# Seven block products in more chunks of a gated feed-forward net, with the activations dealt and turned in contiguous runs

## The chip, the cores and the metric

One core of one Trainium2 chip runs the whole program. The metric is the device time of one execution in microseconds (us). The core has TensorE (PE: matrix products; PEld: the loading of its stationary operand), VectorE (DVE), ScalarE (ACT), GpSimd (POOL) and SyncE (SP, which here only issues DMAs).

## The reference

Two layers; each is a gated feed-forward net, a mixer, cross attention and a second net, each followed by a layer norm. The change touches the four nets (two per layer).

```
D_MODEL = 1024; SEQ = 256; DEPTH = 2; D_FF = 2816

def swiglu(x, w_gate, w_up, w_down):
    return (jax.nn.silu(x @ w_gate) * (x @ w_up)) @ w_down

for l in range(DEPTH):
    h = layer_norm(ALPHA * h + 0.5 * swiglu(h, ffn1_gate[l], ffn1_up[l], ffn1_down[l]), ...)
    ...                                   # mixer: w_in, recurrence, convolution, pooling, w_out
    h = layer_norm(ALPHA * h + mix, ...)
    h = layer_norm(ALPHA * h + cross_attn(h, mem, ca_q[l], ca_k[l], ca_v[l], ca_o[l]), ...)
    h = layer_norm(ALPHA * h + 0.5 * swiglu(h, ffn2_gate[l], ffn2_up[l], ffn2_down[l]), ...)
```

## The kernel before

**Products in three parts.** All data is fp32. Each operand is split into a high part (a cast on ScalarE, line 61, to the type that TensorE takes) and a low part (a subtraction on VectorE, line 62), and a product is the sum of three matmuls: high by high, high by low, low by high (`mm_rows`, lines 130 to 133; every matmul is recorded at line 106). The activations of the net's input stand transposed in `xT` (1024 rows in 8 groups of 128, by 256 tokens), as high and low parts.

**A net in chunks.** `ffn` works through the 2816 hidden columns in five chunks of 512 and a last one of 256 (loop at line 639). A weight tile `raw` holds 1 MB (three of them); `load` fetches it with one DMA from SyncE and splits it in two halves into `whi` and `wlo`, of which there are eight each. An ordinary chunk (`hidden`, line 484) takes two gate and two up loads, so 8 halves, and 96 matmuls of 512 columns; the two token tiles i = 0, 1 get accumulators of their own among four `acc` banks. Then `activate` (ScalarE, line 402) writes SiLU of the gate sums into `sg`, and `gated` (VectorE, line 406) multiplies by the up sums.

**Dealing and turning.** The product with w_down needs the activations transposed. `turn` (line 411) deals `sg` with four DMAs over 32-partition bands into the tile `dealt` (line 415, one buffer), so that VectorE's transposes of 32x32 blocks (line 418, one per token tile) finish the job; then `ah` and `al` take the high and low part. In the transposes both sides are read and written in steps of four elements:

```
nc.vector.transpose(
    d.rearrange("p k (i b) -> p b k i", b=4), x[:, :, i, :].rearrange("p b (j k) -> p b k j", k=4)
)
```

To match this order of rows, w_down is fetched "strewn" (row 4p + k to partition p), save for the last chunk.

**Slabs.** w_down comes in slabs of two 128-row groups (`both`, line 631): 24 matmuls of 512 columns into the four `dn` accumulators, two slabs per chunk. In the loop over c, after chunk c's own products, the second slab of chunk c-2 and the first of chunk c-1 are done. So one slab stands ahead of chunk 2, two stand ahead of chunks 3, 4 and 5. The last slabs are done in `finish`, together with the layer norm.

**The chunk made by seven block products.** In three of the four nets, chunk 3 is made by `by_seven` (line 515): gate and up weights of the chunk, stacked, times the two token tiles form a product of 2 x 2 blocks, which the seven-product scheme of Winograd does with 7 x 12 = 84 matmuls in place of 96, and more additions. `w00` and `w01` are the upper halves of the gate and up weights, `w10` and `w11` the lower halves. The sums w00+w01, w00+w11, w01+w11 and w00+w10 are made in place on VectorE (line 544), each half then split like any weight: 14 halves in all. The sums of x's blocks are made once per net (`blocks_of_x`, line 497) in the tile `spare`, and split into the tiles `kTh` and `kTl`; the same `spare` later takes w00. w01 lies in the tiles of the layer norm's parameters (`lng`, `lnb`), w11 and w10 in two `raw` tiles. The results of the products are combined on VectorE by `put` (line 566). The first net has no such chunk (`early`: its `ffn` pool also builds masks and loads the memory).

**Order.** A planner orders each engine's instructions by priority (the order of the program text) and by its own estimate of when operands and tiles are free; each engine then runs its list in order, each instruction waiting for what it needs. DMA issues on SyncE are such a list too.

**Transposes on TensorE.** `transposed` (line 173) transposes the layer norm's result with an identity matrix `idn` as one operand; after ffn1 the second token tile is reversed with `jdn`.

Of the kernel before, what the change touches and what calls it, by code (L numbers as in the profile page):

```python
# [46 lines left out]
def model(ctx: ExitStack, tc: tile.TileContext, t: dict, out: bass.AP):  # L47
# [16 lines left out]
    def load(src, k0, nk, c0, ncol, fine=False, strewn=False):  # L64

# [4 lines left out]
        for a in range(k0, k0 + nk, step):  # L70
# [4 lines left out]
            for b in range(0, step, part):  # L75
                loads.append(nc.sync.dma_start(
                    raw[:, b : b + part, :],
                    src[:, c0 : c0 + ncol].rearrange("(p k) c -> p k c", p=P)[:, a + b : a + b + part, :]
                    if strewn
                    else src[(a + b) * P : (a + b + part) * P, c0 : c0 + ncol].rearrange("(k p) c -> p k c", p=P),  # L80
                ))
# [71 lines left out]

    jdn = cst.tile([P, P], F32, name="jdn")
# [24 lines left out]
    def load_memory(mp, behind):  # L179
        m = [mp.tile([P, 4, 8, 32], F32, tag="m", name="m", bufs=2) for _ in range(2)]  # L180
# [23 lines left out]
    rows = cst.tile([P, P], F32, name="rows")  # L204
# [10 lines left out]
    def small_parameters(op):  # L215
        nc.gpsimd.memset(rows, 0.0)
# [13 lines left out]
        mf = op.tile([P, NT, len(narrow), 64], F32, name="mf", bufs=1)  # L230
# [61 lines left out]
    def finish(mm, y, scale, gb, last=False, flip=False):  # L292
# [6 lines left out]
        for i in range(NT):  # L299
# [8 lines left out]
            for c in pieces:  # L308
# [6 lines left out]
                else:  # L315
                    mm(
                        i, n, slice(0, 512), None,
                        None if last or not i or not n else lambda: transposed(h[0], 0, xTh, xTl),
# [21 lines left out]
        return lambda: transposed(h[1], 1, xTh, xTl, jdn if flip else idn)  # L340

    def project_back(slabs, late, gb, scale, between=lambda: None):
# [30 lines left out]
        return finish(tail, y, scale, gb)  # L373


    def ffn(l, name, n, pend=None, last=False, early=None):
        gate, up, down = (t[f"{name}_{x}"][l] for x in ("gate", "up", "down"))
        with tc.tile_pool(name="ffn", bufs=2, reuse_waits="tile") as fp:
# [21 lines left out]

            def activate(s, i, og):
                nc.scalar.activation(halves(s[:, i, :]), sums(og), AF.Silu)

            def gated(s, i, ou):
                v = halves(s[:, i, :])
                nc.vector.tensor_tensor(v, sums(ou), v, op=ALU.mult)
# [4 lines left out]
            def turn(s):  # L411
# [4 lines left out]
                for i in range(NT):  # L416
                    d = fp.tile([P, 4, P], F32, tag="up", name="square")
                    nc.vector.transpose(  # L418
                        d.rearrange("p k (i b) -> p b k i", b=4), x[:, :, i, :].rearrange("p b (j k) -> p b k j", k=4)
                    )  # L420
                    split(ah[:, :, tok(i)], al[:, :, tok(i)], d)
                return ah, al

            def first():
# [5 lines left out]
                if pend is None:  # L430
# [8 lines left out]
                    with tc.manual_schedule(engines={E.Activation, E.DVE, E.PE}):  # L439
# [8 lines left out]
                        transposed_half(h[0], 0, 0, xTh, xTl)  # L448
                        busy(1)
                        split(*wg.todo[0])  # L450
                        transposed_half(h[0], 0, 1, xTh, xTl)
# [3 lines left out]
                        transposed_half(h[1], 1, 0, xTh, xTl)  # L455
                        group(1, 0)
                        split(*wg.todo[2])
                        transposed_half(h[1], 1, 1, xTh, xTl)
# [56 lines left out]
            def by_seven(c0, bx):  # L515
                def quarter(m, j, halves_of):
                    for b, r in enumerate(halves_of):
                        n = r.shape[1]
                        k = 4 * j + b * n
                        loads.append(nc.sync.dma_start(  # L520
                            r, m[k * P : (k + n) * P, c0 : c0 + CHUNK].rearrange("(k p) c -> p k c", p=P)
                        ))
                    return [r[:, 2 * h : 2 * h + 2, :] for h in range(2) for r in halves_of[:1]] if n == 4 else halves_of

# [3 lines left out]
                def raw():  # L528
                    return rows_by_columns(wp.tile([P, 2048], F32, tag="raw", name="raw", bufs=3))

                w00 = quarter(gate, 0, [rows_by_columns(
                    fp.tile([P, 4, 4 * P], F32, tag="spare", name="sum", bufs=1).rearrange("p n c -> p (n c)")
                )])
                w01 = quarter(up, 0, [
                    rows_by_columns(wp.tile([P, DM], F32, tag=g, name="raw")) for g in ("lng", "lnb")
                ])
                w11 = quarter(up, 1, [raw()])
                w10 = quarter(gate, 1, [raw()])

                def parts_of(r, plus=None):  # L540
                    hi, lo = [], []
                    for i in range(2):
# [4 lines left out]
                        h, w = (x.rearrange("p (k c) -> p k c", c=CHUNK) for x in (h, w))  # L547
# [14 lines left out]
                def half_sum():  # L562
                    return halves(fp.tile([P, 4, P], F32, tag="up", name="half").rearrange("p k t -> p (k t)"))

                def put(o, a, op, b):
                    nc.vector.tensor_tensor(o, a, b, op=op)

                s = activations()
                g = [halves(s[:, i, :]) for i in range(NT)]
                o = [acc((P, CHUNK)) for _ in range(4)]  # L570
                run(o[0], part_of_x(0, 0), parts_of(w00))
                nc.scalar.copy(g[0], sums(o[0]))
# [3 lines left out]
                put(e, sums(o[1]), ALU.add, g[0])  # L576
                run(o[3], bx[2], parts_of(w01, w11))
                put(g[1], sums(o[3]), ALU.add, e)
                f = half_sum()
                put(f, sums(o[2]), ALU.subtract, g[1])  # L580
                put(e, sums(o[2]), ALU.subtract, e)
# [561 lines left out]
```

## Time and profile before

| | |
|---|---|
| median of 3 runs | 1081.59 us (1081.54 to 1081.89) |
| profiled execution: its time / its span | 1082.44 / 1080.7 us |
| PE busy | 1071.4 us (99%), 6015 matmuls |
| VectorE busy | 908.4 us (84%), 1198 instructions |
| ScalarE busy | 592.8 us (55%) |
| GpSimd busy | 61.0 us (6%) |
| DMA | 231.86 MB, 215 GB/s in the mean |
| mean granted TensorE clock | 0.998 |

The span runs from the first to the last instruction of the profiled execution; its own time has 1.74 us more. "Busy" counts instructions that run, also while matmuls overlap; a matmul of 512 columns is recorded with 380 ns, while the next starts 216 ns after it. In rows of groups the columns are: line, engine, operation, output<-inputs, shape, count, busy us, mean ns of one, and the engine's idle time ahead of them with what ended it. In the chain of work and the timelines a row is: start, duration, engine, line, and xcount of merged instructions.

### The profile page before, as it was taken

The page shows a single profiled execution, that of the slowest core. Times are in us where ns is not written, and L with a number is a line of the kernel's source. Part 1 is how long each engine was busy: PE and PEld are TensorE (multiplying, and loading weights), DVE is VectorE, ACT ScalarE, POOL GpSimd, SP SyncE. Part 2 cuts the span into 40 slices and gives each one's busy share as a digit, 9 for nine tenths or more (in the row PEclk, how much of TensorE's full clock was granted, in tenths as well). Part 3 has the DMA queues.
Part 4 walks back from the last instruction along what each step waited for, and adds up shares of the span by engine and source line. Part 5 has one row for each costly group of instructions (what it writes and reads, how often), then busy time and mean ns, then how long its engine had stood idle before and what let it go on. Part 6 is the DMA issues. An engine that isn't in the chain of part 4 may idle for free.

```text
span 1080.7 us, 15689 instructions
## 1 busy us (share of the span) xinstructions
PE 1071.4 (99%) x6015; PEld 947.5 (88%) x6015; DVE 908.4 (84%) x1198; ACT 592.8 (55%) x828; POOL 61.0 (6%) x113
## 2 busy tenths in 40 slices
PE   9999999999999999999999999999999999999997
PEld 7888888989899888888888888898898998888886
DVE  6678677998988898998697998798989889889885
ACT  6456553766457455556365465456764664645650
POOL 9500001000000000000000000010000000000000
PEclk9999999999999999999999999999999999999999
DMA  9986764754476387288468459656536664773761
GB/s 325 289 293 203 249 223 153 237 196 165 167 263 204 123 295 269 96 275 286 156 234 282 166 166 329 229 165 241 174 122 231 240 228 154 255 253 109 260 236 39
DMA packets 122715, 231.86 MB, mean 215 GB/s; under 512 B 6352, under 2 KB 45552, under 8 KB 117520
## 3 DMA queue, kind: packets, MB, share of 16 engines
q1 hardware_dynamic: 120848, 228.48, 63.1%
q0 software_dynamic: 1216, 1.20, 0.4%
q10 hardware_dynamic: 576, 1.18, 0.3%
q8 instruction: 47, 0.77, 0.3%
q14 instruction: 28, 0.23, 0.1%
HBM read 216.15 MB, written 1.05 MB: 201 GB/s over the span
## 4 chain that ended last, share of the span: by engine, by line
PE 99%; DMA 0%; DVE 0%; issue 0%; DVEq 0%
PE acc L106 65%; PE dn L106 30%; PE acc L170 1%; PE dn L845 1%; DMA h<-in_x_dram 0%; PE dn L904 0%; PE dn L903 0%; PE dn L893 0%; PE acc L969 0%; PE dn L810 0%; PE dn L437 0%; DVE h L334 0%; DVE h L330 0%; DVE st L322 0%; DVE h L314 0%
## 5 line engine op out<-in xcount | busy, mean ns | idle before, releaser
L62 DVE TENSOR_TENSOR wlo<-raw,whi 128x1024 fp32r<-128x1024 f32 (+1 forms) x390 | 460.8, 1207 | 91.0 <-ACT whi L61 81.1
L61 ACT CAST whi<-raw 128x1024 fp32r<-128x1024 f32 (+1 forms) x390 | 391.2, 1040 | 258.3 <-PE dn L106 128.4
L106 PE MATMUL acc<-whi,xT 128*128 128x512 f32 x1192 | 359.7, 380 | 0.0
L106 PEld LDWEIGHTS acc<-whi,xT 128*128 128x128 f32 x1192 | 225.2, 189 | 32.1
L106 PE MATMUL acc<-wlo,xT 128*128 128x512 f32 x596 | 225.9, 379 | 0.0
L106 PE MATMUL acc<-xT,whi 128*128 128x512 f32 x576 | 142.1, 382 | 0.0
L106 PE MATMUL dn<-whi,ah 128*128 128x512 f32 x346 | 131.5, 380 | 0.0
L106 PE MATMUL dn<-wlo,ah 128*128 128x512 f32 x346 | 131.2, 379 | 0.0
L106 PE MATMUL dn<-whi,al 128*128 128x512 f32 x346 | 131.1, 379 | 0.0
L106 PEld LDWEIGHTS acc<-wlo,xT 128*128 128x128 f32 x596 | 112.7, 189 | 15.7
L106 PEld LDWEIGHTS acc<-xT,whi 128*128 128x128 f32 x576 | 104.1, 190 | 11.8
L106 PE MATMUL dn<-whi,xT 128*128 128x512 f32 x288 | 88.8, 382 | 0.0
L106 PEld LDWEIGHTS acc<-xT,wlo 128*128 128x128 f32 x576 | 75.5, 191 | 3.9
L106 PE MATMUL acc<-xT,wlo 128*128 128x256 f32 x576 | 75.9, 275 | 0.0
L106 PEld LDWEIGHTS dn<-wlo,ah 128*128 128x128 f32 x346 | 65.4, 189 | 9.5 <-DVE wlo L62 0.3
L106 PEld LDWEIGHTS dn<-whi,al 128*128 128x128 f32 x346 | 65.4, 189 | 9.3
L106 PEld LDWEIGHTS dn<-whi,ah 128*128 128x128 f32 x346 | 65.4, 189 | 9.1
L418 DVE STREAM_TRANSPOSE square<-dealt 128x512 f32<-128x512 f32 x40 | 62.8, 1645 | 3.8 <-DMA dealt<-sg 3.8
L327 POOL TENSOR_TENSOR rs<-rs,nhalf 128x1 f32<-128x1 f32 x16 | 14.9, 928 | 846.3 <-DVE rs L326 846.3
L106 PEld LDWEIGHTS dn<-whi,xT 128*128 128x128 f32 x288 | 54.7, 190 | 7.8 <-DVE xT L62 0.3
L106 PE MATMUL dn<-wlo,xT 128*128 128x512 f32 x144 | 54.8, 381 | 0.0
L61 ACT CAST ah<-square 128x512 fp32r<-128x512 f32 x40 | 24.6, 619 | 39.7 <-DVE square L418 39.7
(227 smaller groups left out, 1174.0 us busy)
## 6 DMA issues: line engine op xcount, KB each, us to landing
raw<-in_ffn_down_dram SPq DMA_DIRECT2D x44, 1024.0 KB, 5.4
raw<-in_ffn_up_dram SPq DMA_DIRECT2D x41, 1024.0 KB, 6.1
raw<-in_ffn_gate_dram SPq DMA_DIRECT2D x39, 1024.0 KB, 5.1
raw<-in_w_in_dram SPq DMA_DIRECT2D x24, 1024.0 KB, 5.0
dealt<-sg SPq DMA_DIRECT2D x80, 128.0 KB, 3.8
raw<-in_ca_k_dram SPq DMA_DIRECT2D x8, 1024.0 KB, 4.9
raw<-in_w_out_dram SPq DMA_DIRECT2D x8, 1024.0 KB, 4.8
raw<-in_ca_v_dram SPq DMA_DIRECT2D x8, 1024.0 KB, 5.4
```

What stands on the lines that cost most here:

```text
L61: nc.scalar.copy(hi, src)
L62: lows.append(nc.vector.tensor_tensor(lo, src, hi.bitcast(F32), op=ALU.subtract))
L106: nc.tensor.matmul(o, w, x, start=start, stop=stop)
L170: nc.tensor.transpose(pt[:, k, :], src[:, (4 * j + k) * P : (4 * j + k + 1) * P], unit)
L327: nc.gpsimd.tensor_tensor(rs, rs, nhalf[:, 0:1], op=ALU.pow)
L418: nc.vector.transpose(d.rearrange("p k (i b) -> p b k i", b=4), x[:, :, i, :].rearrange("p b (j k) -> p b k j", k=4))
L845: nc.tensor.matmul(o[g, hh, :], kc[:, hh, g], x, start=True, stop=True)
```

## The change

- Chunks 2 and 4 of three nets, and chunk 4 of the first, are made by `by_seven`; x's blocks are made at chunk 1 (in the first net at chunk 3). LN parameters are fetched after the last such chunk.
- `activate` and `gated` work in two instructions of 256 columns per token tile, in an order that needs no steps afterwards. `turn`'s transposes read and write contiguous runs of 32.
- A permuted identity `pdn` (one copy on GpSimd at the start) is used for the transposes ahead of each net's input and output, so that tokens come in the matching order. w_down is no longer strewn; the last chunk's split carries the permutation in its steps.
- In `by_seven`, w00 lies in the tiles `spare0` and `spare1`, w10 in `dealt` and `spare2` (each half with a DMA of its own), w11 in the one `raw` tile. w11's own product now comes fifth, ahead of the two with w10. SiLU and gating come at the end, into a new tile in `spare2`.
- Rows and masks of the small parameters, and the memory's tiles, move into `spare2`, `spare0` and `spare1`.

```
+    pdn = cst.tile([P, P], F32, name="pdn")
+    nc.gpsimd.tensor_copy(pdn.rearrange("p (r b) -> p b r", b=4), idn.rearrange("p (b r) -> p b r", b=4))
...
+            def ordered(v):
+                return v.rearrange("p (a k j) -> p k a j", a=4, j=32)
+
+            def by_two(v, o):
+                o = o.rearrange("p (n a j m) -> p m n a j", n=2, a=4, m=2)
+                return [(ordered(v)[:, 2 * m : 2 * m + 2], o[:, m]) for m in range(2)]
+
             def activate(s, i, og):
-                nc.scalar.activation(halves(s[:, i, :]), sums(og), AF.Silu)
+                for v, o in by_two(s[:, i, :], og):
+                    nc.scalar.activation(v, o, AF.Silu)
 
             def gated(s, i, ou):
-                v = halves(s[:, i, :])
-                nc.vector.tensor_tensor(v, sums(ou), v, op=ALU.mult)
+                for v, o in by_two(s[:, i, :], ou):
+                    nc.vector.tensor_tensor(v, o, v, op=ALU.mult)
...
                     nc.vector.transpose(
-                        d.rearrange("p k (i b) -> p b k i", b=4), x[:, :, i, :].rearrange("p b (j k) -> p b k j", k=4)
+                        d.rearrange("p k (b r) -> p b k r", b=4), x[:, :, i, :].rearrange("p b (k j) -> p b k j", k=4)
                     )
...
-                d = fp.tile([P, 4, 4 * P], F32, tag="spare", name="quarters", bufs=1)
-                q = [d[:, n, :].rearrange("p (k t) -> p k t", t=P) for n in range(4)]
+                d = [fp.tile([P, DM], F32, tag=f"spare{n}", name="quarters", bufs=1) for n in range(2)]
+                q = [d[n // 2].rearrange("p (n k t) -> p n k t", n=2, t=P)[:, n % 2] for n in range(4)]
...
+                def block(m, j, to):
+                    for i in range(2):
+                        k = 4 * j + 2 * i
+                        loads.append(nc.sync.dma_start(
+                            to[i], m[k * P : (k + 2) * P, c0 : c0 + CHUNK].rearrange("(k p) c -> p k c", p=P)
+                        ))
+                    return to
+
+                w00 = block(gate, 0, pieces("spare0", "spare1"))
+                w01 = block(up, 0, pieces("lng", "lnb"))
+                w11 = block(up, 1, whole())
+                w10 = block(gate, 1, pieces("dealt", "spare2"))
...
-                m = acc((P, CHUNK))
-                run(m, part_of_x(0, 1), parts_of(w10))
-                put(g[0], sums(m), ALU.add, g[0])
-                nc.scalar.activation(g[0], g[0], AF.Silu)
-                ...
-                run(m, bx[3], parts_of(w11))
-                put(e, sums(m), ALU.add, e)
-                put(g[0], g[0], ALU.mult, e)
+                o = [acc((P, CHUNK)) for _ in range(3)]
+                run(o[0], bx[3], parts_of(w11))
+                put(e, o[0], ALU.add, e)
+                run(o[1], part_of_x(0, 1), parts_of(w10))
+                put(g[0], o[1], ALU.add, g[0])
+                run(o[2], part_of_x(1, 1), parts_of(w00, w10))
+                put(g[1], o[2], ALU.add, g[1])
+                s = fp.tile([P, NT, CHUNK], F32, tag="spare2", name="sg", bufs=1)
+                for i, u in enumerate((e, f)):
+                    v = ordered(s[:, i, :])
+                    nc.scalar.activation(v, g[i].rearrange("p (k a j) -> p k a j", a=4, j=32), AF.Silu)
+                    nc.vector.tensor_tensor(v, v, u.rearrange("p (k a j) -> p k a j", a=4, j=32), op=ALU.mult)
                 return turn(s)
...
-                split(ah[:, 0:2, :], al[:, 0:2, :], s)
+                for j in range(2):
+                    split(
+                        *(x[:, j, :].rearrange("p (i b r) -> p i b r", i=2, b=4) for x in (ah, al)),
+                        s[:, j, :].rearrange("p (i r b) -> p i b r", i=2, b=4),
+                    )
...
             def slab(c, u):
-                if c < len(chunks) - 1:
-                    w = load(down[c * CHUNK : (c + 1) * CHUNK], 2 * u, 2, 0, DM, strewn=True)
-                else:
-                    w = load(down, c * 4, 2, 0, DM)
+                w = load(down, c * 4 + 2 * u, 2, 0, DM)
...
-            sevens = (3,) if early is None else ()
+            sevens = (2, 4) if early is None else (4,)
...
-                if c == 1 and sevens:
+                if sevens and c == (1 if early is None else min(sevens) - 1):
                     bx = blocks_of_x()
```

More of the change, by code (lines that the diff above doesn't have):

```diff
@@ L179, in load_memory @@
     def load_memory(mp, behind):
-        m = [mp.tile([P, 4, 8, 32], F32, tag="m", name="m", bufs=2) for _ in range(2)]
+        m = [
+            mp.tile([P, DM], F32, tag=f"spare{n}", name="m", bufs=1).rearrange("p (k b j) -> p k b j", k=4, j=32)
+            for n in range(2)
+        ]
         with tc.issue_after(behind.ins):
@@ L215, in small_parameters @@
     def small_parameters(op):
+        spare = op.tile([P, DM], F32, tag="spare2", name="rows", bufs=1)
+        rows = spare[:, 0:P]
         nc.gpsimd.memset(rows, 0.0)
@@ L339, in finish, with project_back @@
                     e.dma_start(out[0, tok(i), c], h[i][:, c])
[L340 to L342 removed]
+        return lambda: transposed(h[1], 1, xTh, xTl, units[1])
+    def project_back(slabs, late, gb, scale, unit, between=lambda: None):
         y = [[acc((P, 512), "dn") for _ in range(2)] for _ in range(NT)]
@@ L515, in by_seven, with whole, pieces @@
             def by_seven(c0, bx):
[L516 to L523, printed above, removed]
                 def rows_by_columns(r):
                     return r.rearrange("p (k c) -> p k c", c=CHUNK)
[L528 to L538, printed above, removed]
+                def whole():
+                    r = rows_by_columns(wp.tile([P, 2048], F32, tag="raw", name="raw", bufs=3))
+                    return [r[:, 0:2, :], r[:, 2:4, :]]
+                def pieces(*tags):
+                    pools = {"lng": wp, "lnb": wp}
+                    return [
+                        rows_by_columns(pools.get(g, fp).tile([P, DM], F32, tag=g, name="raw", bufs=1)) for g in tags
+                    ]
+                def block(m, j, to):
[9 more added lines that the diff above has]
+                w10 = block(gate, 1, pieces("dealt", "spare2"))
                 def parts_of(r, plus=None):
```

60 lines of the change are left out of this document (26 added, 34 removed).

## The prediction

> **What bounds the kernel now.** I read the page first: the busy times, then the chain that ended last.
>
> ```profile
> span 1080.7 us, 15689 instructions
> PE 1071.4 (99%) x6015; PEld 947.5 (88%) x6015; DVE 908.4 (84%) x1198; ACT 592.8 (55%) x828; POOL 61.0 (6%) x113
> PE 99%; DMA 0%; DVE 0%; issue 0%; DVEq 0%
> ```
>
> TensorE is the bound twice over: busy for 99% of the span, and 99% of the chain. A product less is time less, as long as nothing makes TensorE wait. VectorE, at 84%, is the engine that could. The chain in order of time, for the second half of layer 0, shows how the products follow each other.
>
> ```profile
> 380.99 33.67 PE acc L106 x156
> 414.66 5.18 PE dn L106 x24
> 419.84 20.72 PE acc L106 x96
> 440.56 10.36 PE dn L106 x48
> 450.92 18.13 PE acc L106 x84
> 469.05 10.36 PE dn L106 x48
> 479.41 20.72 PE acc L106 x96
> ```
>
> Each piece begins where the last one ends, so there is no wait. The 96 products are an ordinary chunk (216 ns each), the 84 are the block chunk, and 48 "dn" products are two slabs of w_down. Chunk 2 begins at 419.84 after one slab (5.18 us), chunk 3 at 450.92 after two. The table by stretches (columns: stretch, its length, then busy time of PE, PEld, DVE, ACT, POOL) shows VectorE's spare time: first an ordinary chunk of the first net, then chunks 2, 3 and 4 of this one.
>
> ```profile
> 118.31:149.40 31.09, 31.09 (x146) 27.23 (x145) 19.94 (x19) 14.68 (x17) 0.00 (x0) 1.00 0.66 219
> 419.84:450.92 31.08, 31.08 (x145) 27.22 (x145) 28.10 (x26) 14.72 (x16) 0.00 (x0) 1.00 0.57 192
> 450.92:479.41 28.49, 28.49 (x133) 24.95 (x133) 28.07 (x30) 17.48 (x21) 0.00 (x0) 1.00 0.59 196
> 479.41:510.49 31.08, 31.08 (x145) 27.22 (x145) 25.12 (x23) 17.25 (x20) 0.00 (x0) 1.00 0.89 311
> ```
>
> One block chunk already fills VectorE through its own stretch (28.07 of 28.49 us) and most of the one before, where its first operands are made ahead. So the question is not the total; it is whether the block chunk's operands are ready in time when block chunks come twice per net.
>
> **Products removed.** A block chunk takes 18.13 us where an ordinary one takes 20.72: 2.59 us less. Three nets go from one to two block chunks and the first net from none to one: four more, 4 x 2.59 = **10.36 us** off the path. The profiled execution took 1082.44 us, 1.74 more than its span and 0.85 above the median of the runs, 1081.59. Without any new wait it would take 1082.44 - 10.36 = 1072.08; by the median, 1071.23.
>
> **VectorE's work.** Its order of work in chunk 3 gives the price of each operation when they stand back to back (start to next start).
>
> ```profile
> 443.48 2.35 DVE L544 TENSOR_TENSOR sum<-sum,raw 128x1024 f32<-128x1024 f32 x2
> 445.75 1.22 DVE L544 TENSOR_TENSOR raw<-raw 128x1024 f32<-128x1024 f32 x1
> ...
> 451.42 3.10 DVE L418 STREAM_TRANSPOSE square<-dealt 128x512 f32<-128x512 f32 x2
> 454.40 1.18 DVE L62 TENSOR_TENSOR wlo<-raw,whi 128x1024 fp32r<-128x1024 f32 x1
> 455.51 1.27 DVE L62 TENSOR_TENSOR al<-square,ah 128x512 fp32r<-128x512 f32 x2
> 456.71 3.48 DVE L62 TENSOR_TENSOR wlo<-raw,whi 128x1024 fp32r<-128x1024 f32 x3
> 460.11 2.34 DVE L62 TENSOR_TENSOR wlo<-sum,whi 128x1024 fp32r<-128x1024 f32 x2
> 462.38 0.67 DVE L566 TENSOR_TENSOR half<-acc,sg 128x512 f32<-128x512 f32 x1
> 462.99 2.34 DVE L62 TENSOR_TENSOR wlo<-raw,whi 128x1024 fp32r<-128x1024 f32 x2
> 465.25 0.67 DVE L566 TENSOR_TENSOR sg<-acc,half 128x512 f32<-128x512 f32 x1
> ```
>
> A weight half's low part costs 1.13 us (3.40 for three), a block sum the same, a 512-wide operation 0.60, a stepped transpose 1.49 (2.98 for two). A block chunk has 14 low parts, 8 sums and 9 short operations (30.3 us) where an ordinary one has 8 low parts and 2 short ones (10.2). Four more: +80 us; x's blocks in the first net, 12 short operations, +7. What the new turn gives back is read from three transposes of the same size:
>
> ```profile
> L418 DVE STREAM_TRANSPOSE square<-dealt 128x512 f32<-128x512 f32 x40 | 62.8, 1645 | 3.8 <-DMA dealt<-sg 3.8
> L406 DVE TENSOR_TENSOR sg<-acc,sg 128x512 f32<-128x512 f32 x34 | 22.4, 683 | 0.0
> L127 DVE TENSOR_TENSOR sums<-acc,sums 128x256 f32<-128x256 f32 x32 | 13.3, 419 | 2.5 <-ACT sums L126 2.5
> L980 DVE STREAM_TRANSPOSE yr<-dealt 128x512 f32<-128x512 f32 x4 | 4.7, 1287 | 0.0
> L1054 DVE STREAM_TRANSPOSE square<-dealt 128x512 f32<-128x512 f32 x6 | 4.2, 705 | 0.0
> ```
>
> L418 steps by four elements in reading and in writing, L980 in writing alone, L1054 in neither, as the new turn does: 0.94 us less each, 40 times, -38 us (0.62 back to back). [...] Gating in two halves costs 2 x 419 ns for 683, 26 times: +4 us. VectorE's total goes to about 908 + 80 + 7 - 38 + 4 = 961 us, 90% of the new span: it does not bind as a total. ScalarE, at 55%, takes 24 more casts and the halved activations unseen.
>
> **Chunk 4 of each net.** Chunk 3 of before is its model: the same lead, with two slabs ahead. There the last of the 14 low parts ended at 465.3 (462.99 + 2.34); TensorE first needs it 13/14 into the chunk, at 450.92 + 16.84 = 467.76, so 2.5 us were to spare. The cheaper turn in that stretch adds 1.7 and the gating in halves takes 0.3. Since chunk 3 is ordinary again, VectorE has 55 us of work for the 59.6 us of a block and an ordinary chunk with their slabs (block: 30.3, turn 2.4, four slab halves 4.5; ordinary: low parts 9.1, gating 1.4, turn 2.4, slabs 4.5). I take no wait. In the first net VectorE is busy for only 19.94 of 31.09 us, so x's blocks (7 us) fit: none there either.
>
> **Chunk 2 of three nets** is the tight place. The lead comes from eight halves of high and low parts, and it opens five ordinary halves and a slab before the chunk, 18.1 us ahead, at 401.7.
>
> ```profile
> 400.63 0.68 DVE L62 TENSOR_TENSOR kTl<-quarters,kTh 128x512 fp32r<-128x512 f32 x1
> ...
> 404.94 2.36 DVE L62 TENSOR_TENSOR wlo<-raw,whi 128x1024 fp32r<-128x1024 f32 x2 [2.49 <-ACT whi L61]
> ```
>
> VectorE is up to date then: it idles for 2.49 us after 402.45. Against chunk 4's margin of 3.9 us, chunk 2 must also take the turn of chunk 0 (2.5 us) in this stretch, and its second half of w00 waits for x's last quarter, read until 401.2: up to 2 us of idling. Margin: 1.4 to -0.6 us.
>
> The other limit is w10, whose first half now lies where the turn of chunk 1 lands, so SyncE can't ask for it before that turn is done. Behind it in SyncE's queue stand loads of chunk 3, which begins 28.5 us after chunk 2.
>
> ```profile
> 416.71 2.63 SPq L415 DMA_DIRECT2D dealt<-sg  x4
> 442.45 2.61 SPq L415 DMA_DIRECT2D dealt<-sg  x4
> dealt<-sg SPq DMA_DIRECT2D x80, 128.0 KB, 3.8
> raw<-in_ffn_up_dram SPq DMA_DIRECT2D x6, 512.0 KB, 4.0
> sum<-in_ffn_gate_dram SPq DMA_DIRECT2D x3, 1024.0 KB, 7.3
> L61 ACT CAST whi<-raw 128x1024 fp32r<-128x1024 f32 x382 | 386.6, 1049 | 258.3 <-PE dn L106 128.4 <-PE acc L106 42.3 <-DMA raw<-in_ffn_up_dram 29.1
> ```
>
> Dealing chunk 1 starts at 416.71. At the earliest the deal has landed 5.8 us later (2.0 to the last issue, 3.8 to land), 422.5; in chunk 3, VectorE came to the transposes 9.0 us after the deal began (442.45 to 451.42), which would be 425.7. Two transposes 1.24, the half of w10 4.0 (a transfer of its size) to 7.3 us (the slowest row), cast 1.05, low part 1.13: ready between 422.5 + 7.4 = 429.9 and 425.7 + 10.7 = 436.4. It is needed after five of the seven products, at 419.84 + 5 x 2.59 = 432.79: from 2.9 us early to 3.6 late. I take the later start, which the trace shows, and the transfer of this size: 433.1, 0.3 late. The sum w00+w10 behind it loses some 0.7 more (sum, cast and low part, 3.3, for 2.59 of products), and VectorE's thin margin 0.5: **1.5 us in each of three nets**, bounds 0 and about 4.3. In sum 1081.59 - 10.36 + 4.5 = **1075.7 us**.
>
> **Edits at nothing.** The w_down loads come in 4 KB rows instead of 8; w_out's 4 KB rows land in 4.8 us, w_down's in 5.4.
>
> ```profile
> raw<-in_ffn_down_dram SPq DMA_DIRECT2D x44, 1024.0 KB, 5.4
> raw<-in_w_out_dram SPq DMA_DIRECT2D x8, 1024.0 KB, 4.8
> 4.66 1.09 PE L170 MATMUL acc<-idn,h 128*128 128x128 f32 x4 [0.63 <-DMA h<-in_x_dram]
> ```
>
> The permuted identity is one 128x128 copy on GpSimd ahead of these transposes, which wait for x until 4.52 us; it is hidden unless it ends later. The stepped split of the last chunk adds 1 to 3 us of VectorE's time where no block chunk stands. The LN parameters are asked for one chunk later, and are first used after the last chunk and the last slabs.
>
> **Rivals.**
> First, VectorE at its limit, and no change. Every hand-over between ScalarE and VectorE leaves a gap once there is no lead, and the idling before chunk 2's operands comes at its upper end. At 3.5 us per net, 10.4 us, the gain is gone: 1081.6. For it: 28.07 of 28.49 us. Against: chunk 3's 2.5 us to spare. Chance 0.13.
>
> Second, w10 late, and slower. With the slow transfer w10's first half is 3.6 us late and the sum behind it 0.7: 4.3 per net, 12.9, so 1084.1; with another 1.5 us in SyncE's queue or in VectorE's order 1088. It decides from 3.45 us per net (10.36 / 3). For it: w10 of before lay in a raw tile, free long ahead, and now it must wait for the turn just done. Against: w11's product now goes ahead of it, and 4.0 us is what its size takes. Chance 0.20.
>
> Third, the turn gets no cheaper, so the change doesn't do what it says. Both forms cost 1.49 us; chunk 2 has two turns, 4 x 0.87 = 3.5 us more, so 1.5 + 3.5 = 5.0 per net: 1086.2. The three rows speak against it. Chance 0.05. [...]
>
> **How the numbers follow.** 0.2% (2.2 us) is about what a measurement of this kernel can tell from no change. My forecast, waits of 0 to 2.7 us per net, gives 1071.2 to 1079.4, chance 0.62, all faster. The first rival is the chance of the same, the other two make slower: 0.25. The range goes from 1071 (no wait at all) to 1086: it leaves out the upper part of the last two rivals, about 0.1.
>
> **What would show it.** TensorE should have 48 matmuls fewer. Transposes in the turn at about 0.70 us, VectorE near 90%. In the chain, chunk 4's pieces without gaps, 84 products in 18.13 us; chunk 2's 84 products stretched by 0 to 3 us, with the gap before its sixth and seventh products, and the wait of ScalarE's cast there put down to w10's DMA. I am wrong if chunk 4 waits too, if chunk 2 waits at its first four products (then it is the lead, not w10), or if the first net loses time.

## The result and the profile after

The changed kernel takes 1109.28 us (median; 1106.66 to 1110.86), the kernel before 1081.74 (1081.54 to 1081.89): a ratio of 1.0252, 95% interval 1.023 to 1.0274. Forecast were 1075.7 us, with a range of 1071 to 1086: the change is 27.5 us slower where a gain of 5.9 was expected. The profiled execution took 1108.3 us with a span of 1106.6, 25.9 more than the span before. The head of its page, the first line of its chain, two of its groups of instructions, and one of its DMA groups:

```profile
span 1106.6 us, 15828 instructions
PE 1076.4 (97%) x5967; PEld 939.4 (85%) x5967; DVE 962.5 (87%) x1324; ACT 621.0 (56%) x890; POOL 62.1 (6%) x114
PE 70%; DVE 22%; issue 4%; DMA 3%; ACT 1%; SPq 0%; DVEq 0%; ACTq 0%
L433 DVE STREAM_TRANSPOSE square<-dealt 128x512 f32<-128x512 f32 x40 | 26.0, 687 | 4.3 <-DMA dealt<-sg 4.3
L420 DVE TENSOR_TENSOR sg<-acc,sg 128x256 f32<-128x256 f32 x52 | 18.9, 414 | 0.5 <-PE acc L103 0.5
raw<-in_ffn_down_dram SPq DMA_DIRECT2D x44, 1024.0 KB, 6.3
```

All that was counted came out as counted: 48 matmuls fewer, the turn's transposes at 687 ns, VectorE at 962.5 us where 961 was worked out. VectorE's share is only 87%. Yet the chain, of which TensorE had 99%, is now VectorE's for 22%: not for want of VectorE's time in sum, but of its results at certain moments. The table by stretches shows which (stretch, length, then busy time of PE, PEld, DVE, ACT, POOL, granted clock, DMA share, GB/s): chunk 4 of the first net with its two slabs, then chunks 2, 3 and 4 of layer 0's second net with theirs, and last a piece out of the middle of that chunk 4.

```profile
117.49:158.98 41.49, 33.63 (x134) 25.06 (x132) 37.85 (x40) 23.03 (x26) 0.00 (x0) 0.96 0.38 117
429.81:459.87 30.06, 29.29 (x133) 24.54 (x132) 27.16 (x31) 17.33 (x21) 0.00 (x0) 1.00 0.61 179
459.87:490.95 31.08, 31.08 (x145) 27.22 (x144) 26.60 (x28) 16.55 (x21) 0.00 (x0) 1.00 0.76 268
490.95:525.25 34.30, 30.85 (x133) 25.91 (x132) 30.37 (x34) 18.52 (x22) 0.00 (x0) 0.95 0.46 142
511.93:515.34 3.41, 3.19 (x8) 2.57 (x9) 2.55 (x5) 3.21 (x4) 0.00 (x0) 0.50 0.00 0
```

A block chunk with two slabs should take 28.49 us (18.13 + 10.36). The first net's takes 13.0 more; in layer 0's second net chunk 2 takes 1.6 more and chunk 4 5.8 more. In the other two nets the same stretches have 2.2 and 5.9, and 1.5 and 5.9. So the span comes out as -10.4 (products) + 13.0 (first net) + 5.3 (chunk 2, three nets) + 17.7 (chunk 4, three nets) = 25.6, of 25.9. The last row is part of chunk 4's price: TensorE waits for 0.5, 2.1 and 0.8 us, and from within the third wait on its granted clock is 0.50 for 3.41 us, in which the matmuls start 0.43 us apart in place of 0.216; that costs some 1.7 us more (half of 3.41).

The chain of work through that chunk 4 (start, duration, what; the shorter pieces are left out) shows where in the chunk it stalls:

```profile
480.76 10.36 PE dn L103 x48
491.12 9.08 PE acc L103 x42
501.99 1.22 DVE wlo L62
504.94 1.20 DVE half L583 x2
508.55 1.15 DVE raw L561
510.87 1.24 DVE wlo L62
512.15 2.50 PE acc L103 x5
```

The slabs ahead run without a gap. The operands of the first six of its seven products are all ready in time, so TensorE's first wait is at the second matmul of the seventh, x's block times (w00 + w10). In VectorE's own order (start, duration, line, what) that sum stands far back:

```profile
503.72 1.21 DVE L561 TENSOR_TENSOR raw<-raw 128x1024 f32<-128x1024 f32 x1
504.86 0.68 DVE L583 TENSOR_TENSOR half<-acc,sg 128x512 f32<-128x512 f32 x1
505.46 0.68 DVE L583 TENSOR_TENSOR half<-acc,half 128x512 f32<-128x512 f32 x1
506.12 1.22 DVE L62 TENSOR_TENSOR wlo<-raw,whi 128x1024 fp32r<-128x1024 f32 x1
507.27 0.68 DVE L583 TENSOR_TENSOR half<-acc,half 128x512 f32<-128x512 f32 x1
507.87 0.68 DVE L583 TENSOR_TENSOR sg<-acc,sg 128x512 f32<-128x512 f32 x1
508.46 1.22 DVE L561 TENSOR_TENSOR raw<-raw 128x1024 f32<-128x1024 f32 x1
510.87 1.23 DVE L62 TENSOR_TENSOR wlo<-raw,whi 128x1024 fp32r<-128x1024 f32 x1 [1.19 <-ACT whi L61]
```

There is no idle time until 509.7: VectorE is simply late. The second half's sum ends at 509.7, ScalarE's cast and the low part follow, and TensorE, which should have had it at 507.8 (490.95 + 13 x 1.295), gets it at 512.1.

### The profile page after: what moved, and what is told of

It is laid out like the page before. It is cut to its first block, busy times and chain, and to the rows that moved or that the text cites. A ratio compares the mean times of both kernels' runs of the same rounds, so it can differ in the third digit from the quotient of the medians.

```text
span 1106.6 us, 15828 instructions
## 1 busy us (share of the span) xinstructions
PE 1076.4 (97%) x5967; PEld 939.4 (85%) x5967; DVE 962.5 (87%) x1324; ACT 621.0 (56%) x890; POOL 62.1 (6%) x114
## 4 chain that ended last, share of the span: by engine, by line
PE 70%; DVE 22%; issue 4%; DMA 3%; ACT 1%; SPq 0%; DVEq 0%; ACTq 0%
PE acc L103 42%; PE dn L103 26%; DVE wlo L62 9%; DVE raw L561 3%; DMA raw<-in_ffn_gate_dram 2%; DVE half L583 1%; ACT whi L61 1%; DVE quarters L518 1%; DVE h L338 1%; DVE sg L420 1%; PE acc L170 1%; DVE kTl L62 1%; DVE square L433 1%; DVE quarters L526 1%; DMA dealt<-sg 1%
## 5 line engine op out<-in xcount | busy, mean ns | idle before, releaser
L61 ACT CAST whi<-raw 128x1024 fp32r<-128x1024 f32 (+1 forms) x438 | 435.4, 1041 | 273.8 <-PE dn L103 94.0
L62 DVE TENSOR_TENSOR wlo<-raw,whi 128x1024 fp32r<-128x1024 f32 (+1 forms) x438 | 515.6, 1208 | 68.6 <-ACT whi L61 64.4
L103 PE MATMUL acc<-whi,xT 128*128 128x512 f32 x1032 | 316.6, 382 | 9.7 <-ACT whi L61 9.7
L103 PEld LDWEIGHTS acc<-whi,xT 128*128 128x128 f32 x1032 | 196.0, 190 | 39.4 <-ACT whi L61 12.0
L103 PE MATMUL acc<-wlo,xT 128*128 128x512 f32 x516 | 199.0, 386 | 8.4 <-DVE wlo L62 8.3
L103 PEld LDWEIGHTS acc<-wlo,xT 128*128 128x128 f32 x516 | 98.0, 190 | 28.6 <-DVE wlo L62 15.2
L561 DVE TENSOR_TENSOR raw<-raw 128x1024 f32<-128x1024 f32 x56 | 66.2, 1217 | 3.0 <-DMA raw<-in_ffn_gate_dram 2.8
L103 PE MATMUL acc<-whi,kTh 128*128 128x512 f32 x112 | 43.2, 386 | 2.3 <-ACT whi L61 2.3
```

The costliest lines, as they stand in the source:

```text
L61: nc.scalar.copy(hi, src)
L62: lows.append(nc.vector.tensor_tensor(lo, src, hi.bitcast(F32), op=ALU.subtract))
L103: nc.tensor.matmul(o, w, x, start=start, stop=stop)
L561: nc.vector.tensor_tensor(r[i], r[i], plus[i], op=ALU.add)
```

## The experiments

Two readings were possible. **Theory W**: the first half of w10 lies in `dealt`, where the turn's DMAs land, so it and its sum come late. **Theory V**: VectorE cannot make two block chunks' operands in one net. For the first net **theory T**: x's blocks and w00 use the tiles in which the memory lies until 95 us, so w00 comes late. Times before in the shared runs were 1081.66 to 1082.15 us.

### Without the first net's block chunk

```
-            sevens = (2, 4) if early is None else (4,)
+            sevens = (2, 4) if early is None else ()
```

> The first net keeps five ordinary chunks; all else is the changed kernel. In the changed kernel's profile its first net takes 10.7 us more than before (168.9 us from its first full chunk to the turn of its result, against 158.2), and the three others 5.0 us more each. If the first net's loss is the block chunk's own, it goes altogether: 1108.3 - 10.7 = 1097.6, and the three others stay as they are. If part of it comes from the other edits of the first net (memory tiles that share, gating in halves), some of it stays: 1098 to 1103, and chunks 3 and 4 show it.

1098.22 us, ratio 1.0153 (1.0138 to 1.0168). The first net's loss is the block chunk's own; its other edits cost nothing. The other nets stall as in the changed kernel (30.0 and 34.4 us for chunks 2 and 4 of layer 0's second net). This is the base of the next runs, save where one is said to have a block chunk in its first net.

### One block chunk in three nets: chunk 4, or chunk 2

The same line with `(4,)`, and with `(2,)`, in place of `(2, 4)`.

> The first net has no block chunk, the three others one, chunk 4; as many products as before. Theory W (w10 lies in the tile of the turn, so its sum with w00, the last of the block's operands, comes late): chunk 4 keeps its stall of 5.4 us and the 0.4 us behind it, 1081.6 + 3 x 5.8 = 1099. Theory V (VectorE cannot make the operands of two block chunks in one net): one alone runs in 18.1 us, and the time is that of before, 1081.6.

> The first net has no block chunk, the three others one, chunk 2. Both theories leave chunk 2 its wait of about 1.4 us per net, since nothing of a second block chunk lies ahead of it: 1081.6 + 4.2 = 1085.8. Theory W puts the wait in the sixth and seventh products; if it is VectorE's work of the second block chunk that pushes into chunk 2, it is gone: 1081.6.

Chunk 4 alone: 1081.80 us, ratio 0.9999 (0.999 to 1.0008); chunk 2 alone: 1086.88, ratio 1.0046 (1.0031 to 1.0061). Chunks 3 and 4 of the first of these two kernels:

```profile
450.39:481.47 31.08, 31.08 (x145) 27.22 (x144) 25.11 (x26) 14.70 (x18) 0.00 (x0) 1.00 0.42 140
481.47:509.96 28.49, 28.49 (x133) 24.95 (x132) 27.06 (x30) 17.24 (x21) 0.00 (x0) 1.00 0.56 177
```

With w10 in the turn's tile as in the changed kernel, chunk 4 has no stall at all when chunk 2 is ordinary. Theory W is not enough for chunk 4. Chunk 2 loses 1.4 to 2.3 us per net even alone. Apart, the two cost nothing and 5.1 us; together 24.2 (1098.2 - 1081.8 + 3 x 2.59): they harm each other.

### w10 in a weight tile

```
-                w10 = block(gate, 1, pieces("dealt", "spare2"))
+                w10 = block(gate, 1, whole())
```

> The changed kernel with w10 in a tile of the weights' own, as before, in all four nets. Theory W: the stalls of the last product go, 5.8 us in chunk 4 and 1.4 us in chunk 2 of three nets, 21.6 us; in the first net only the part at the sixth and seventh products (about 4 of 13 us): about 1084. Theory V: the stalls stay, 1105 to 1109. A rival to both: the third weight tile that w10 now takes delays the loads of the next chunk, and the stall moves behind the block chunk.

1100.97 us, ratio 1.0175 (1.0158 to 1.0192): neither number. This kernel has the changed kernel's first net, so it is to be compared with 1109.28. Chunk 2 loses 1.0 us in each net and chunk 4 3.4 to 5.1, so w10's place has a part in it, the smaller one. The spread in chunk 4 is the clock: TensorE waits for 2.6 us in it in layer 0's second net and in the net after, but the granted clock falls to 0.50 for 3.41 us in the later one alone, and the same waits cost 3.4 us without the fall and 5.1 with it.

### Chunk 2 without sums; block chunks 1 and 4

```
-                        if plus is not None:
+                        if plus is not None and c0 != 2 * CHUNK:
```

and `sevens = (1, 4)` with x's blocks made after chunk 0.

> First net plain, as in the run that took 1098.2. In chunk 2 of the other three nets the eight in-place sums of weight blocks are left out, so its products use the plain blocks and the output is not the reference's; the number of products stays. That takes 8 x 1.13 = 9 us of VectorE's work away just ahead of and in chunk 2. Theory V (VectorE comes out of chunk 2 with no lead, gives its weight tiles back late, then idles for late loads, and so has not the time for chunk 4): chunk 2 loses its wait of 1.4 us and chunk 4, which is untouched, its stall of 6.2 us: 1098.2 - 3 x 7.6 = 1075.4. If chunk 4's stall is its own (order of its sums, its tiles), only chunk 2's wait goes: 1094.

> First net plain; the two block chunks of the other three nets are 1 and 4 in place of 2 and 4, so two ordinary chunks lie between them, and x's blocks are made one chunk earlier. Theory V: chunk 4 runs in 18.1 us as it does alone, since VectorE has another 31 us to catch up; chunk 1 has less lead than chunk 2 had and waits more, 2 to 8 us in each net: 1098.2 - 22.8 + 6 to 24 = 1081 to 1099. If the stall of chunk 4 does not depend on the distance, it stays at 23.5 us in the profile, and the whole takes 1100 to 1118.

Without the sums: 1104.36 us, ratio 1.0204 (1.0178 to 1.023), above both numbers of the expectation. This speaks against theory V as it was put: VectorE had 9 us less to do, yet chunk 2 lost 2.1 to 3.3 us and chunk 4 5.2 to 6.6. With 1 and 4: 1121.76, ratio 1.0369 (1.0353 to 1.0384), slower than either case expected. Chunk 4 is clean there in all three nets, so distance cures it, as theory V says; the whole is slower because the stretch up to the end of chunk 1, with LN and x's blocks right ahead, grows to 52.6 us at a mean granted clock of 0.90.

```profile
380.65:433.27 52.62, 44.53 (x174) 34.13 (x172) 48.19 (x58) 26.44 (x33) 0.00 (x0) 0.90 0.48 145
494.99:523.48 28.49, 28.49 (x133) 24.95 (x132) 27.76 (x32) 17.20 (x21) 0.00 (x0) 1.00 0.54 169
```

The two results together gave **theory L**: what chunk 4 lacks is the lead, the halves that lie ready ahead, and chunk 2 may use it up in either of two ways. The lead can be worked out: a block chunk has 14 halves, of which TensorE needs one every 1.295 us (six matmuls); the moment of need, less the end of the half's low part in VectorE's timeline, is its lead (below zero, it comes late). In the last net of each profile, in us, for the first half, the first half of w10, and the last two (w00 + w10):

```
                                 chunk 2                     chunk 4
                          first  w10  last two       first  w10  last two
before (chunk 3)             -    -     -    -        15.6  2.3   2.0  2.1
chunk 4 alone                -    -     -    -        15.6  5.0   2.9  2.5
first net plain, 2 and 4  15.6  0.2  -1.3 -2.3        11.7  1.8  -0.9 -4.3
w10 in a weight tile      15.6  2.4   2.1 -1.3        12.0  2.3  -0.4 -3.8
chunk 2 without sums      15.6 -2.2  -2.5 -2.3        12.0  2.3  -0.3 -3.8
the two edits together    15.1  5.5   4.0  3.6        14.3  3.9   3.7  0.8
half tiles                11.1 -3.8  -4.1 -3.9        14.0  3.9   0.6  0.2
```

(In the row of before the columns of w10 and "last two" hold the eleventh and the last two of its 14 halves; w11 came last there.) A full lead is 15.6 us, and a block chunk spends 13 of it. Chunk 2 begins with a full lead and still ends at -2.3, by the late w10 as well as by the sums: taking one away leaves the other. Chunk 4 then begins with 12 us, which is 1 to 2 too little (it ends 4 short; a part of that is the place of its last sum, tested below). Why 31 us of chunk 3 do not restore the lead is seen on SyncE's queue. The loads of chunk 3's gate in the changed kernel, whose chunk 3 begins at 459.87, and in that with chunk 4 alone, whose chunk 3 begins at 450.39:

```profile
437.59 0.37 SPq L75 DMA_DIRECT2D raw<-in_ffn_gate_dram  x1
446.60 2.70 SPq L547 DMA_DIRECT2D raw<-in_ffn_gate_dram  x2
452.45 0.37 SPq L75 DMA_DIRECT2D raw<-in_ffn_gate_dram  x1
```

```profile
421.90 5.55 SPq L75 DMA_DIRECT2D raw<-in_ffn_gate_dram  x2
```

The second one is asked for 7 us ahead of the chunk instead of 23, because a weight tile comes free only when VectorE has made its low parts (the one ahead of this request ended at 452.38). It lands 6.0 us later, at 458.49, and 0.1 us behind that ScalarE's cast begins. The profile names TensorE as what ended this wait; in the kernel whose first net is plain it puts the same wait (6.91 us) down to the load itself. There are three such tiles, so a late VectorE makes late loads; that the late loads in turn keep it late is read from these rows, and the half tiles below bear on it. ScalarE's row (start, duration, the wait ahead of it):

```profile
458.59 2.00 ACT L61 CAST whi<-raw 128x1024 fp32r<-128x1024 f32 x2 [6.68 <-PE dn L103]
```

And VectorE's waits (total, times, longest) from 429.81 to 490.95:

```profile
DVE wlo L62 <- ACT whi L61: 6.5, 4, 3.9
DVE raw L561 <- DMA raw<-in_ffn_gate_dram: 0.8, 1, 0.8
```

That is 7.3 us of idling, just ahead of a chunk that is 4.3 us late. Idle time alone would not have told this: in the kernel with chunk 4 alone VectorE waits 7.3 us in chunk 3 too, but there because its lead is full.

### GpSimd for the sums

`nc.gpsimd.tensor_tensor` in place of `nc.vector.tensor_tensor` at line 561.

> First net plain, block chunks 2 and 4; the in-place sums run on GpSimd, which is idle in these nets, so VectorE has 8 x 1.13 = 9 us less per block chunk. Theory V: if a sum takes GpSimd no more than about twice VectorE's 1.13 us and leaves VectorE its pace, both stalls go and the time is 1081.8 - 3 x 2.59 = 1074. No row shows what such a sum costs on GpSimd, nor whether the two engines hinder each other: with 4 us or more for a sum, or with VectorE slowed, 1085 to 1110.

1142.45 us, ratio 1.056 (1.0542 to 1.0577). GpSimd's row, and VectorE's low parts beside it:

```profile
L561 POOL TENSOR_TENSOR raw<-raw 128x1024 f32<-128x1024 f32 x48 | 135.6, 2838 | 257.3 <-DVE wlo L62 215.1 <-DMA raw<-in_ffn_gate_dram 41.2
L62 DVE TENSOR_TENSOR wlo<-raw,whi 128x1024 fp32r<-128x1024 f32 x10 | 16.0, 1648 | 5.6 <-ACT whi L61 5.6
```

This is slower than both cases of the expectation. A sum takes 2.84 us in the mean (2.35 at the least), inside the bound of 4 that the expectation gave, but it lies in the path between two casts (ScalarE waits 87.0 us for such sums, in 27 waits), and in chunk 2 (the second row is from that stretch) VectorE's low parts take 1648 ns in the mean where 1217 is usual: seven of the ten take 1.21 us, and the three that start while a sum runs on GpSimd take 2.3 to 3.4. A sum on GpSimd takes 2838 ns against 1217 on VectorE, 2.3 times as long; the least is 1.9 times.

### The first net, one chunk earlier

```
-                if c == 2 and early is not None:
-                    with tc.issue_after(lows[-1].ins):
-                        for f in rest:
-                            f()
```

moved into the branch for c == 1, and x's blocks made at c == 2 in place of 3.

> The changed kernel, but in the first net the memory and the small parameters are worked up in chunk 1 in place of chunk 2, and x's blocks are made in chunk 2 in place of chunk 3; the other nets as they are. Theory T (the memory's tiles hold the two tiles in which x's blocks are made and into which w00 is loaded, so w00 arrives only as chunk 4 begins): w00 is there early, chunk 4 of the first net runs in 18.1 us as it does alone in the other nets, and 13 us go: 1109.3 - 13 = 1096. If VectorE has too much to do in chunks 3 and 4 of the first net, whatever the tiles: 1105 to 1109.

1098.78 us, ratio 1.0153 (1.0138 to 1.0168). Theory T holds: the first net's 13.0 us are gone. The time falls by 10.5 only, because the other nets lose 2.4 more than in the changed kernel; in two of their chunks 4 the clock is at 0.50 for 6.83 us in place of 3.41. Want of VectorE's time is not what was cured: in the chunk ahead VectorE is busier here (30.35 of 31.08 us) than in the changed kernel (26.58). The last reading of the memory's tiles, the requests for w00 and the deal of chunk 3 in the changed kernel, and ScalarE's wait behind them:

```profile
94.07 0.70 DVE L198 STREAM_TRANSPOSE turned<-m 128x512 f32<-128x512 f32 x1
...
104.00 0.37 SPq L547 DMA_DIRECT2D raw<-in_ffn_gate_dram  x1
109.36 2.89 SPq L430 DMA_DIRECT2D dealt<-sg  x4
112.62 7.47 SPq L547 DMA_DIRECT2D raw<-in_ffn_gate_dram  x2
119.13 1.21 ACT L61 CAST ah<-square 128x512 fp32r<-128x512 f32 x2 [8.29 <-DVE square L433]
```

x's blocks follow the memory in its tiles and w00 follows them, so w00's second half is asked for at 112.62, 5 us ahead of the chunk and after the deal, whose four parts take 6.7 to 7.8 us to land while these loads are under way, where 4.3 is the median of all deals (6.65 us of it on the chain); and ScalarE's casts of w00 stand behind the turn of chunk 3. One chunk earlier both halves are asked for at 92.34 (SyncE's row), and chunk 4 with its slabs is clean (table by stretches):

```profile
92.34 1.48 SPq L547 DMA_DIRECT2D raw<-in_ffn_gate_dram  x2
```

```profile
118.39:146.88 28.49, 28.49 (x133) 24.95 (x132) 27.04 (x30) 17.29 (x21) 0.00 (x0) 1.00 0.58 179
```

### Both causes away, and faster loads

The first of these runs has no sums in chunk 2, and w10 in a weight tile in both block chunks. The second splits the three weight tiles of 1 MB into six of 512 KB, each with a load of its own (`bufs=6`). The third adds w10 in two such tiles and the earlier first net.

> First net plain; in chunk 2 of the other three nets the in-place sums are left out (the output is not the reference's), and w10 lies in a tile of the weights' own. Theory L (chunk 2 ends with no operands made ahead, because two things each use them up: the cast of w10 that stands in ScalarE's queue until the turn is done, and 9 us of sums; the lead then comes back at the pace of the late loads, too slowly for chunk 4): with both away chunk 2 runs in 18.1 us and chunk 4 loses nothing or little: 1098.2 - 3 x 7.6 = 1075.4, up to 1081. If chunk 4's stall is its own, only chunk 2's wait goes: 1094.

> First net plain, block chunks 2 and 4; every weight is loaded in pieces of 512 KB into six half tiles, in place of 1 MB into three, in the same memory. Theory L: a half tile is free sooner and its load lands sooner, so chunk 3's loads are not late, VectorE does not idle for 6 us there, and the 6.2 us of chunk 4 shrink to 0 to 3 us; chunk 2's wait of 1.4 us stays: 1098.2 - 10 to 19 = 1079 to 1088. If it is VectorE's amount of work that chunk 4 lacks, and not the loads, nothing changes: 1096 to 1100. A third way: twice as many requests on SyncE make the loads later, over 1100.

> The half tiles, w10 in two of them, the first net's block chunk with x's blocks and the memory one chunk earlier, and block chunks 2 and 4 in the other nets: all four remedies, the output as the reference's. Theory L: the first net takes 1.6 us less than before, the others keep at most 2 us of chunk 2's wait and 0 to 3 us of chunk 4's: 1081.7 - 1.6 + 3 x (-2.6 + 0 to 5) = 1072 to 1087, at its middle 1078, faster than before.

Both causes away: 1074.66 us, ratio 0.9934 (0.9921 to 0.9947), within a microsecond of theory L's 1075.4. Chunks 2, 3 and 4:

```profile
419.01:447.50 28.49, 28.49 (x133) 24.95 (x132) 26.30 (x29) 18.77 (x22) 0.00 (x0) 1.00 0.77 242
447.50:478.58 31.08, 31.08 (x145) 27.22 (x144) 27.17 (x29) 15.89 (x21) 0.00 (x0) 1.00 0.62 219
478.58:507.14 28.56, 28.56 (x133) 24.87 (x132) 28.25 (x32) 18.05 (x21) 0.00 (x0) 1.00 0.59 182
```

Chunk 4 loses 0.1, 0.1 and 0.7 us. Its own w10 lies in a weight tile here, but it did so too in the run of that edit alone, where chunk 4 lost 3.4 to 5.1. In these nets the two kernels differ in chunk 2's sums alone, so what cures chunk 4 was done to chunk 2: what chunk 4 lacked was handed on from there. Half tiles: 1088.98 us, ratio 1.0066 (1.0053 to 1.0079), a microsecond above what was expected, and for a mixed reason:

```profile
418.99:450.63 31.64, 29.69 (x134) 24.51 (x132) 30.64 (x34) 18.32 (x22) 0.00 (x0) 1.00 0.63 195
481.71:510.90 29.19, 28.98 (x133) 24.79 (x132) 28.16 (x31) 17.52 (x21) 0.00 (x0) 1.00 0.58 171
```

Chunk 4 is nearly clean, as theory L wanted, but chunk 2 loses 3.2 to 5.2 us, since it begins with a lead of 11.1 in place of 15.6. Though chunk 2 ends further behind (-3.9 against -2.3), chunk 4 begins with 14.0 us against 11.7, and VectorE idles for 4.9 us in layer 0's chunks 2 and 3 against 7.3 in the changed kernel: this is what late loads as the cause would give. The third run missed: 1093.70 us, ratio 1.0095 (1.008 to 1.011), where 1072 to 1087 was expected. Chunk 4 is clean in all nets, but chunk 2 loses 6.5 to 7.4 us (its lead begins at 9.5, and the clock is at 0.50 for 6.83 us in each). Why the half tiles shorten the lead ahead of chunk 2 was not tried and stays open.

### w10's halves swapped; the last sum first

`pieces("spare2", "dealt")` for w10, with whole and with half tiles; and, by itself, w00 += w10 of the second halves issued right after the fourth product.

> First net plain, block chunks 2 and 4, whole weight tiles; the first half of w10 lies in the spare tile, which is free early, and the second in the turn's tile. If w10's late first half is what makes ScalarE's queue stand in chunk 2, its casts behind it start 1 to 3 us earlier, chunk 2 loses 0 to 1 us in place of 1.5, and chunk 4 with the better lead 2 to 4 us in place of 5.9: 1098.2 - 3 x (2.4 to 5.4) = 1082 to 1091. If VectorE's sums set the wait, nothing changes: 1096 to 1099.

> The same swap with the half weight tiles, and the first net's block chunk with the memory and x's blocks one chunk earlier. Half tiles alone left chunk 4 clean and took 1089.0 with a plain first net, so chunk 2 cost 15 us in three nets there. If the late first half of w10 is most of that, chunk 2 loses 1 to 3 us per net: 1081.7 - 10.4 + 3 to 9 = 1075 to 1081, faster than before. If the sums are, 1085 to 1089.

> First net plain, block chunks 2 and 4; the sum of the second halves of w00 and w10, whose data are there early, is issued ahead of the block's last products in place of behind them, so that in VectorE's order it no longer stands behind four short operations. If its place is half of the matter, chunk 4 loses 1 to 3.5 us in place of 5.9, and the drop of TensorE's clock goes with it: 1098.2 - 3 x (2.4 to 4.9) = 1083 to 1091. If the missing lead alone decides, the sum taken ahead only makes other operands late by the same 1.1 us: 1096 to 1099.

Swapped: 1094.29 us, ratio 1.0118 (1.0103 to 1.0133), between the two cases of the expectation. Chunk 2 keeps its 1.5 to 2.4 us and chunk 4 loses 3.4 to 5.0: the late first half of w10 alone was not chunk 2's wait. With half tiles 1092.05, ratio 1.0094 (1.0077 to 1.0111), above both expectations, again by chunk 2 (6.2 to 7.0 us). The last sum first: 1092.31, ratio 1.0098 (1.0081 to 1.0115), between the cases too; chunk 4 loses 3.2 to 4.8 us in place of 5.8 to 7.0, chunk 2 as with the first net plain. TensorE's waits in chunk 4 fall from between 3.1 and 3.4 us to 2.6, so the place of one sum in VectorE's order is about a fifth of them; the rest of the difference is the clock, which fell for two stretches of 3.41 us in place of four. The other waits went only where the lead was larger. How a lead that is 1 to 2 us short still ends 3 short with the sum in front was not followed further.

### The version to keep

`sevens = (4,)` in all nets, with the earlier first net.

> One block chunk, chunk 4, in every net, the first net's with the memory and x's blocks one chunk earlier. The two parts are known to run alone: 1081.8 for chunk 4 alone in three nets, and 1.6 us less for the first net (156.6 us against 158.2). In sum 1080.2; no theory expects a stall.

1080.63 us, ratio 0.999 (0.9981 to 0.9998). It is 0.1% faster than before, less than the 0.2% that the prediction set as its bound; no other version with the reference's whole computation was faster.

## Why the prediction was wrong, point by point

- **Products removed**, 10.36 us: right. Where no wait stands, the block chunk takes 18.13 us.
- **VectorE's work**, 961 us and no bound as a total: right in the sum, and the sum was the wrong question. The transposes measured 687 ns in contiguous runs, where they had taken 1645 with steps of four elements, so the third rival falls.
- **"Chunk 4 of each net ... the same lead, with two slabs ahead ... I take no wait."** This step failed, and cost 17.7 us (some 5 of them by the three falls of the clock). The slabs are the same, the lead is not: chunk 3 of before starts with 15.6 us, chunk 4 of after with 11.7, and a block chunk spends 13. The step balanced VectorE's 55 us of work against 59.6 us of time, as if VectorE could work throughout; it idled for 7.3 us of the 61 between the two starts, behind loads that its own lateness had delayed. It also took over the margin of a chunk whose last operand was a plain block, where the last is now a sum: 3.9 us were worked out, and alone chunk 4 shows 2.5.
- **"In the first net VectorE is busy for only 19.94 of 31.09 us, so x's blocks (7 us) fit: none there either."** This step failed, and cost 13.0 us. The time was there; the tiles were not. The memory's share of `spare0` and `spare1` was in the diff, and was not followed to the moment at which w00 could be asked for.
- **Chunk 2**, 1.5 us: right in size (1.6, 2.2, 1.5), in the place (the last product), and in w10's ask behind the turn. The size was in part luck: it was put down to w10 for the most part, yet with w10 in a weight tile 1.0 us stays, with the halves of w10 swapped 1.5 to 2.4, and without the sums 2.1 to 3.3; only both edits together end it. And I saw the price only in chunk 2; that it ends with an empty lead, and what that does to the next chunks, is what decided.
- **The rivals.** The first is nearest in kind (hand-overs leave gaps "once there is no lead") with a price of 3.5 us per net; the runs show 7.7 (23.0 / 3), and none of the three rivals had the first net in it. None reached the measured time. Of the signs of being wrong that were named, two came true: chunk 4 waits, and the first net loses time.
- **Edits at nothing**: w_down's 4 KB rows land in 6.3 us in place of 5.4, but in the kernel with chunk 4 alone they cost nothing; the first net's other edits cost nothing.

## What to carry to other kernels

When a stage lives on a lead (buffers filled ahead), count what the stage spends of it and what the stages between give back, not the sum of an engine's work against the time. An engine that falls behind can free its input tiles late, so that its loads come late and it idles in the midst of its own backlog (here a load was asked for 7 us ahead of its chunk in place of 23, and VectorE idled for 7.3 us). And when tiles are shared, follow each tile from its last reader to the next request for it, in order of time: an idle engine does not help data that cannot yet be asked for.

## What the hardware showed that was not expected

TensorE's granted clock fell to 0.50 for 3.41 us four times in the changed kernel: in the first net's stall (from 122.81 us) and in each of the three chunks 4 (from 511.93, 689.42 and 1054.65), though the longest single wait in each of these chunks was 2.14 us (in layer 0's from 508.75 to 510.89). In the 3.41 us ahead of the four falls TensorE was busy for 1.01, 0.71, 1.68 and 0.73 us. What brings a fall about was not shown: the first net's waits, 7.8 us in sum between 117.49 and 148.60, came with one, and with w10 in a weight tile 2.6 us of waits came with one in one net and with none in another. So the same waits cost 3.4 us there, or 5.1 with the fall, and such falls moved several of the losses above.

Subtractions on VectorE took longer beside GpSimd's sums: in the stretch above, those that start while a sum runs take 2.3 to 3.4 us in place of 1.21. What holds them up was not shown.
